# One layer, two mixers: h transposed through DRAM instead of on TensorE, and modulation row 5 at another place

## The chip, the cores and the metric

The kernel runs on one core of a Trainium2 chip. A core has five engines that work side by side: TensorE (PE; its weight loads are listed as PEld), VectorE (DVE), ScalarE (ACT), GpSimd (POOL) and SyncE (SP). SP only issues transfers here, one after the other, and waits wherever a transfer's data or its buffer isn't ready. Each engine works through its own row of instructions in a fixed order; semaphores hold an instruction until what it needs is there. The metric is the device time of one execution in microseconds (us).

## The reference, cut to what matters

One transformer-like layer over 512 tokens of width 1024, in fp32:

```python
mod = silu(c) @ w_ada + b_ada                  # nine modulation rows of 1024
sh1, sc1, g1, sh2, sc2, g2, sh3, sc3, g3 = split(mod, 9)

u = rms_norm(x, ffn1_norm_g) * (1 + sc1) + sh1
x = x + 0.5 * g1 * swiglu(u, ffn1_w_in, ffn1_w_out)

u = rms_norm(x, mix_norm_g) * (1 + sc2) + sh2
z = u @ w_mix + b_mix                          # q,k,v,o,i,f of the mLSTM; q,k,v,f of attention; two gates
h_m = mlstm_chunkwise(silu(causal_conv(q_m, k_m)), v_m, i_m, f_m)      # 4 heads of 256
y_a = sigmoid(o_m) * rms_norm(h_m, mlstm_norm_g)
y_b = forgetting_attention(q_f, k_f, v_f, f_f)                         # 16 heads of 64
merged = sigmoid(g_a) * (y_a @ w_branch_a) + sigmoid(g_b) * (y_b @ w_branch_b)
x = x + g2 * (merged @ w_out)

u = rms_norm(x, ffn2_norm_g) * (1 + sc3) + sh3
x = x + 0.5 * g3 * swiglu(u, ffn2_w_in, ffn2_w_out)
```

Row 5 of the modulation (counted from 0) is `g2`, which is first needed where the product with `w_out` is added to x.

## The kernel before

**Products.** Every fp32 product is made of three: operands are split into a high part (`uh`, `wh`) and a rest (`ul`, `wl`), and `mm3` (lines 140 to 142) adds high by high, rest by high, high by rest. One weight tile of 128 columns goes through these stations: SP loads it (`raw`, line 105, 512 KB, a ring of three buffers that all weights and all `w_ada` loads share), ACT rounds it to `wh` (line 115), DVE subtracts to get `wl` (line 117), and PE uses it in 24 products of 128x512 (`gemm_stat`). The first and second product of each three or the first two of a tile can start once `wh` is there; the third needs `wl`.

**Stages.** Start and first feed-forward part (to about 380 us), the qk products with the convolutions (`qk_conv`, about 400 to 480), the four mLSTM heads (`mlstm_w`, `mlstm_h`, to about 550), sixteen attention heads in steps `fox_s`, `fox_p`, `fox_o` (to about 815), the two branches (`branch`, to about 920), the product with `w_out`, and the second feed-forward part. Between the steps of the heads and of attention other work is laid in by a generator that `advance` moves on: value and key products, fourteen of the gate products (`gate`), and during the last four attention heads the eight `y_a(m)`. What sets the order on each engine is the order in which this is written, and a scheduler that places every instruction by priority when the program is built; the order is fixed before it runs.

**h of the mLSTM.** `mlstm_h` leaves h of a head as 128 tokens by 256 columns (`hn`, two token blocks to a tile), scales it by its norm on DVE (line 1128, sixteen times) and stores it to DRAM (`h_d`, line 1129). `y_a(m)` needs it the other way round, columns on partitions: it loads 128 columns of all tokens (`ht`, line 1342), transposes four blocks on PE (line 1345), scales on ACT (line 1347) and multiplies with the tanh of the output gate `th` (line 1340) on DVE (line 1348).

**Transposes through DRAM.** The attention's q and k already go another way: DVE transposes every 32x32 block in place (line 1169), the tile is stored, and `blocks` (line 1134) loads it in four transfers of 64 KB that put the blocks at their transposed places.

**Modulation rows.** `ada_row(v, ...)` makes one row in eight steps: a step loads 128 rows of `w_ada` (512 KB through the `raw` ring) and multiplies and adds them on DVE (line 315 first, then 317). Six short pieces (`fold`, `high`, `low`, `total`, `bias`, `put`) follow, each due a number of ticks later; `later` keeps them, `tick` counts. Before, the generator `self.ada` makes rows 5, 6 and 7: row 5 in the second half of `y_a`, a tick and a step at each of its two pauses from m = 4 on, rows 6 and 7 in the branches.

**Gates.** `gate` writes the tanh of a gate (`tg`, line 1364) and stores it to `g_d` (line 1366); the branches load it back (line 1374). `post(n, f)` keeps a piece of program back for n steps of `advance`.

**Start.** In the first product's loop the modulation of block n is summed in pieces; `mod_first(n)` is its first multiply, on ACT (line 838), or on DVE if its second argument is true (line 836). `lo()` in `u_part` makes the `ul` of a norm (line 281).

Of the kernel before, what the change touches and what calls it, by code (L numbers as in the profile page):

```python
# [20 lines left out]
P = 128  # L21
# [26 lines left out]
class Layer:  # L48
# [35 lines left out]
    def advance(self, gen, n):  # L84
        for _ in range(n):
            next(gen, None)
            for p in self.posts[:]:
                p[0] -= 1
                if p[0] < 0:
                    self.posts.remove(p)  # L90
                    p[1]()
# [179 lines left out]
    def u_part(self, hf, b, k, pool, G, sh, act, eng):  # L271
# [7 lines left out]
        else:  # L279
            pin(nc.vector.tensor_scalar(uf, ps, G[:, k:k + 1], sh[:, k:k + 1], op0=MUL, op1=ADD))  # L280
        return lambda: pin(eng.tensor_tensor(self.ul[k][:, c], uf, self.uh[k][:, c], op=SUB))  # L281

# [495 lines left out]
    def start(self, st, tp):  # L778
# [131 lines left out]
        for k in range(NK):  # L910
# [13 lines left out]
            if n < NK:  # L924
# [7 lines left out]
                if n + 1 < NK:  # L932
                    mod(n + 1, 6, 8)
                    w_hi(n + 1)
                    if n + 2 < NK:
                        mod_first(n + 2)
                    w_lo(n + 1)
# [165 lines left out]
    def mlstm_h(self, h, ip):  # L1103
        nc, sp = self.nc, self.sp
        (Wh, Wl), (vh, vl) = self.W[h], self.vt[h]
        ss = sp.tile([P, NT], F32, name=self.nm("hs"), tag="hs", bufs=2)
        hs = []
        for tb in range(NT):
            if tb % 2 == 0:
                h2 = ip.tile([P, 2, 256], F32, name=self.nm("hn"), tag="bc", bufs=4)  # L1110
            ps = self.tbank()
            for sb in range(tb + 1):
# [14 lines left out]
        for tb in range(NT):  # L1127
            nc.vector.tensor_scalar(hs[tb], hs[tb], r[:, tb:tb + 1], None, op0=MUL)
            nc.sync.dma_start(self.h_d[tb * P:(tb + 1) * P, h * 256:(h + 1) * 256], hs[tb])

# [194 lines left out]


    def y_a(self, m, ap, ip):
        nc = self.nc
        def step():
            if m >= NK // 2:  # L1330
                self.tick()
                next(self.ada)
        ps = self.gbank()
        w = self.w_stat(self.A["w_mix"][0], OM + m * P)
        self.gemm_stat(ps, w, 0, T, range(0, 4))
        step()
        yield
        self.gemm_stat(ps, w, 0, T, range(4, 8))
        th = self.tmp(ip, "th")
        nc.scalar.activation(th, ps, AF.Tanh, scale=0.5, bias=self.hom[:, m:m + 1])  # L1340
        ht = ip.tile([P, NT, P], F32, name=self.nm("ht"), tag="tok", bufs=4)
        nc.sync.dma_start(ht, self.h_d[:, m * P:(m + 1) * P].rearrange("(b p) n -> p b n", p=P))
        b = self.tbank()
        for tb in range(NT):
            nc.tensor.transpose(b[:, tb * P:(tb + 1) * P], ht[:, tb, :], self.ident)
        ya = ap.tile([P, T], F32, name=self.nm("ya"), tag="qk", bufs=16)
        nc.scalar.activation(ya, b, AF.Copy, scale=self.hmg[:, m:m + 1])
        nc.vector.scalar_tensor_tensor(ya, th, 1.0, ya, op0=ADD, op1=MUL)
        self.ya[m] = ya
        step()  # L1350
        yield


    def gate(self, m, i, ip, th=None):
# [10 lines left out]
        if not keep:  # L1365
            nc.sync.dma_start(self.g_d[8 * i + m], th)
        yield
# [26 lines left out]
    def run(self):  # L1394
# [140 lines left out]
        row = lambda: yp.tile([2, 512], F32, name=self.nm("br"), tag="qk", bufs=16)  # L1535
        self.ada = (s for v in (5, 6, 7) for s in self.ada_row(v, new, row, self.gbank))
        with tc.tile_pool(name="gates", bufs=1) as mp:
# [3 lines left out]
            for m in range(4, 8):  # L1541
                ps = self.gbank()
                self.gemm_stat(ps, self.w_stat(w_mix, m * P), 0, T)
                if m == 7:
# [3 lines left out]
        with tc.tile_pool(name="att", bufs=1) as ip:  # L1548
# [149 lines left out]
```

## Time and profile before

| | |
|---|---|
| median of 3 runs | 1315.86 us (1315.68 to 1318.32) |
| the profiled execution | 1316.01 us |
| its span, first to last instruction | 1314.2 us |
| granted TensorE clock, mean | 0.999 |
| PE busy | 1296.7 us |
| DVE busy | 960.1 us |
| ACT busy | 631.6 us |

How to read the rows shown below. In the page's first part, each engine has its busy time, its share of the span and its number of instructions. A row of the windows has the stretch in us, then for each engine its busy time and how many instructions lie there, then the clock, the share of the DMA engines and GB/s. A row of the chain has the start, the length and what it was: each piece is what released the one after it. A row of the waits reads "who, line <- for whom: us in total, times, longest". A row of the timeline has start, length, engine, line and operation, out<-in, and in brackets how long the engine stood idle before it and for what. A row of one line or tile has the count, then the shortest, median and longest duration in ns, then the first and last start. In a row of the groups the mean of one is given in ns behind the busy time.

### The profile page before, as it was taken

How to read it: one execution, taken by the hardware profiler on the slowest of the kernel's cores; microseconds unless marked ns; L12 is line 12 of the kernel's file. 1: busy time of each engine (PE TensorE's matmuls, PEld its weight loads, DVE VectorE, ACT ScalarE, POOL GpSimd, SP SyncE). 2: the span in 40 equal slices, each digit the busy share in tenths (PEclk: the TensorE clock that was granted, in tenths of full speed). 3: DMA queues.
4: the chain of work that ended last, by engine and by line, in shares of the span. 5: the costliest groups of instructions: out<-in, count | busy, mean ns of one | idle time of the engine just before them, and what ended most of it. 6: DMA issues, size and time to landing. Idle time of an engine off the chain costs nothing.

```text
span 1314.2 us, 17824 instructions
## 1 busy us (share of the span) xinstructions
PE 1296.7 (99%) x6297; PEld 1087.8 (83%) x6297; DVE 960.1 (73%) x1747; ACT 631.6 (48%) x1056; POOL 36.9 (3%) x57
## 2 busy tenths in 40 slices
PE   7999999999999999999999999999999999999998
PEld 6788888887889888888888878878898888888887
DVE  6877777578688687888888679677557556635787
ACT  5633232355476555567575766234372223223642
POOL 1000000000010101000000000003000000000000
PEclk9999999999999999999999999999999999999999
DMA  9999888465845334535545467777639777634574
GB/s 289 277 328 302 298 275 275 152 192 160 299 134 141 110 107 130 165 117 137 141 115 168 109 188 203 216 247 234 189 101 322 265 246 262 215 103 133 171 266 148
DMA packets 231563, 260.49 MB, mean 198 GB/s; under 512 B 40545, under 2 KB 172289, under 8 KB 231473
## 3 DMA queue, kind: packets, MB, share of 16 engines
q1 hardware_dynamic: 231088, 259.27, 63.3%
q8 instruction: 50, 0.82, 0.3%
q14 instruction: 41, 0.33, 0.1%
q0 software_dynamic: 320, 0.06, 0.0%
q10 hardware_dynamic: 64, 0.02, 0.0%
HBM read 220.43 MB, written 38.87 MB: 197 GB/s over the span
## 4 chain that ended last, share of the span: by engine, by line
PE 83%; DVE 6%; DMA 5%; ACT 3%; issue 2%; SPq 1%; DVEq 0%; ACTq 0%
PE g L142 21%; PE g L141 21%; PE g L140 21%; PE t L140 4%; PE t L141 4%; PE t L142 4%; DMA raw<-in_w_branch_a_dram 2%; PE g L922 1%; DMA raw<-in_w_mix_dram 1%; DVE wl L117 1%; ACT wh L115 1%; PE t L1320 1%; DVE acc L317 1%; PE t L1290 1%; PE t L1261 1%
## 5 line engine op out<-in xcount | busy, mean ns | idle before, releaser
L115 ACT ACTIVATE wh<-raw 128x1024 fp32r<-128x1024 f32 (+2 forms) x246 | 249.0, 1016 | 376.1 <-PE g L141 107.2
L117 DVE TENSOR_TENSOR wl<-raw,wh 128x1024 fp32r<-128x1024 f32 (+2 forms) x246 | 288.0, 1173 | 164.2 <-ACT wh L115 142.3
L140 PE MATMUL g<-uh,wh 128*128 128x512 f32 (+1 forms) x880 | 340.7, 387 | 0.0
L141 PE MATMUL g<-ul,wh 128*128 128x512 f32 (+1 forms) x880 | 339.4, 386 | 0.8 <-DVE ul L281 0.8
L142 PE MATMUL g<-uh,wl 128*128 128x512 f32 (+1 forms) x880 | 339.4, 386 | 0.0
L141 PEld LDWEIGHTS g<-ul,wh 128*128 128x128 f32 x880 | 165.4, 188 | 33.7 <-DVE ul L281 1.0
L142 PEld LDWEIGHTS g<-uh,wl 128*128 128x128 f32 x880 | 165.3, 188 | 33.7
L140 PEld LDWEIGHTS g<-uh,wh 128*128 128x128 f32 x880 | 165.3, 188 | 32.6 <-issue 0.6
L140 PE MATMUL g<-wh,uh 128*128 128x512 f32 (+1 forms) x256 | 96.6, 379 | 0.0
L141 PE MATMUL g<-wl,uh 128*128 128x512 f32 (+1 forms) x256 | 96.5, 377 | 0.1
L142 PE MATMUL g<-wh,ul 128*128 128x512 f32 (+1 forms) x256 | 96.5, 377 | 0.0
L317 DVE SCALAR_TENSOR_TENSOR acc<-raw,ccol,acc 128x512 f32<-128x512 f32 (+1 forms) x70 | 66.8, 975 | 38.3 <-DMA raw<-in_w_ada_dram 38.1
L140 PE MATMUL t<-wh,A 128*128 128x512 f32 x176 | 68.6, 390 | 0.0
L141 PE MATMUL t<-wl,A 128*128 128x512 f32 x176 | 68.6, 390 | 0.0
L142 PEld LDWEIGHTS g<-wh,ul 128*128 128x128 f32 x256 | 48.2, 188 | 9.1
L141 PEld LDWEIGHTS g<-wl,uh 128*128 128x128 f32 x256 | 48.2, 188 | 8.9 <-DVE wl L117 0.5
L140 PEld LDWEIGHTS g<-wh,uh 128*128 128x128 f32 x256 | 48.1, 188 | 8.4
L142 PE MATMUL g<-yh,wl 128*128 128x512 f32 x128 | 50.1, 391 | 1.2 <-DVE wl L117 1.2
L141 PE MATMUL g<-yl,wh 128*128 128x512 f32 x128 | 49.9, 390 | 0.0
L140 PE MATMUL g<-yh,wh 128*128 128x512 f32 x128 | 49.8, 389 | 0.0
L1272 ACT ACTIVATE S<-S,mn 128x128 f32<-128x128 f32 (+1 forms) x64 | 35.5, 555 | 22.1 <-DVE mn L1264 11.0
L433 ACT ACTIVATE A<-E 128x768 fp32r<-128x768 f32 x22 | 18.6, 845 | 50.9 <-DVE E L432 50.9
(366 smaller groups left out, 2235.5 us busy)
## 6 DMA issues: line engine op xcount, KB each, us to landing
raw<-in_ffn_w_in_dram SPq DMA_DIRECT2D x82, 512.0 KB
raw<-in_w_ada_dram SPq DMA_DIRECT2D x56, 512.0 KB
raw<-in_w_mix_dram SPq DMA_DIRECT2D x46, 512.0 KB
sa<-in_ffn_w_out_dram SPq DMA_DIRECT2D x22, 512.0 KB
sb<-in_ffn_w_out_dram SPq DMA_DIRECT2D x44, 256.0 KB
ws<-sa SPq DMA_DIRECT2D x22, 512.0 KB
ws<-sb SPq DMA_DIRECT2D x44, 256.0 KB
raw<-ws SPq DMA_DIRECT2D x44, 256.0 KB
```

The source lines that it names most:

```text
L115: nc.scalar.activation(hi, src, AF.Copy)
L117: self.last_lo = nc.vector.tensor_tensor(lo, src, hi, op=SUB)
L140: pin(mm(ps, lh, rh, start=start, stop=False))
L141: pin(mm(ps, lh, rl, start=False, stop=False))
L142: self.last_mm = pin(mm(ps, ll, rh, start=False, stop=stop))
L317: nc.vector.scalar_tensor_tensor(a, r[:, s], c, a, op0=MUL, op1=ADD)
L433: nc.scalar.activation(A1[:, 0:3, :], E[:, 0:3, :], AF.Copy)
L922: pin(nc.tensor.matmul(acc_ps[b], (wl if p == 1 else wh)[:, b % 2, s], self.ul[k] if p == 2 else self.uh[k], start=k == 0 and p == 0, stop ...
L1261: nc.tensor.matmul(ps[:, :w], q[:, s], k[:, :w], start=True, stop=False)
L1272: nc.scalar.activation(S[:, ws], S[:, ws], AF.Exp, scale=-1.0, bias=m, accum_out=sm[:, qb:qb + 1])
L1290: tr = lambda b, c, qb, kb: nc.tensor.transpose(b[:, c:c + P], S[:, P_OFF[qb] + kb * P:P_OFF[qb] + (kb + 1) * P], self.ident)
L1320: nc.tensor.matmul(po[:, q0:], vt[:, kb, i, :], Px[:, o:o + T - q0], start=n == 1, stop=n == 8)
```

## The change

h of the mLSTM is scaled on ACT, transposed on DVE in 32x32 blocks (two token blocks at a time, 128x512), and stored so; `ht_load` brings it with `blocks`, one m ahead of its use, and `y_a` has no PE transposes. Row 5 gets a generator of its own, `early`: four steps beside the qk products m = 4 to 7, four in the mLSTM heads 0 and 1; `advance` now ticks on each step that was really taken. Its sums lie in `yb[5]` to `yb[7]`, which are not yet in use there. A gate's store, h's store and ya's last operation are posted one step later. At the start, for n = 1, `mod_first` goes to DVE and comes after `w_lo`. `lo()` notes `last_ul`, so that the first multiply of row 8 is placed behind the last `ul` of the second feed-forward part's norm.

```diff
@@ advance
-            next(gen, None)
+            if next(gen, self) is not self:
+                self.tick()
@@ u_part
-        return lambda: pin(eng.tensor_tensor(self.ul[k][:, c], uf, self.uh[k][:, c], op=SUB))
+        def lo():
+            self.last_ul = pin(eng.tensor_tensor(self.ul[k][:, c], uf, self.uh[k][:, c], op=SUB))
+        return lo
@@ start
                     w_hi(n + 1)
+                    if n == 1:
+                        w_lo(n + 1)
+                        mod_first(n + 2, True)
+                        continue
                     if n + 2 < NK:
                         mod_first(n + 2)
                     w_lo(n + 1)
@@ mlstm_h
-            nc.vector.tensor_scalar(hs[tb], hs[tb], r[:, tb:tb + 1], None, op0=MUL)
-            nc.sync.dma_start(self.h_d[tb * P:(tb + 1) * P, h * 256:(h + 1) * 256], hs[tb])
+            nc.scalar.activation(hs[tb], hs[tb], AF.Copy, scale=r[:, tb:tb + 1])
+            if tb % 2:
+                t = h2s[tb // 2].rearrange("p b n -> p (b n)")
+                nc.vector.transpose(t, t)
+                self.post(1, lambda t=t, b=tb - 1: nc.sync.dma_start(
+                    self.h_d[b * P:(b + 2) * P, h * 256:(h + 1) * 256].rearrange("(b p) n -> p b n", p=P),
+                    t.rearrange("p (b n) -> p b n", b=2)))
@@ y_a
+    def ht_load(self, m, ip):
+        t = ip.tile([P, T], F32, name=self.nm("ht"), tag="tok", bufs=4)
+        self.blocks(t, self.h_d[:, m * P:(m + 1) * P])
+        self.ht.append(t)
+
     def y_a(self, m, ap, ip):
         nc = self.nc
-        def step():
-            if m >= NK // 2:
-                self.tick()
-                next(self.ada)
+        if m == 0:
+            self.ht = []
+            self.ht_load(0, ip)
         ps = self.gbank()
         w = self.w_stat(self.A["w_mix"][0], OM + m * P)
         self.gemm_stat(ps, w, 0, T, range(0, 4))
-        step()
         yield
+        if m + 1 < NK:
+            self.ht_load(m + 1, ip)
         self.gemm_stat(ps, w, 0, T, range(4, 8))
         th = self.tmp(ip, "th")
         nc.scalar.activation(th, ps, AF.Tanh, scale=0.5, bias=self.hom[:, m:m + 1])
-        ht = ip.tile([P, NT, P], F32, name=self.nm("ht"), tag="tok", bufs=4)
-        nc.sync.dma_start(ht, self.h_d[:, m * P:(m + 1) * P].rearrange("(b p) n -> p b n", p=P))
-        b = self.tbank()
-        for tb in range(NT):
-            nc.tensor.transpose(b[:, tb * P:(tb + 1) * P], ht[:, tb, :], self.ident)
         ya = ap.tile([P, T], F32, name=self.nm("ya"), tag="qk", bufs=16)
-        nc.scalar.activation(ya, b, AF.Copy, scale=self.hmg[:, m:m + 1])
-        nc.vector.scalar_tensor_tensor(ya, th, 1.0, ya, op0=ADD, op1=MUL)
+        nc.scalar.activation(ya, self.ht[m], AF.Copy, scale=self.hmg[:, m:m + 1])
+        self.post(1, lambda: nc.vector.scalar_tensor_tensor(ya, th, 1.0, ya, op0=ADD, op1=MUL))
         self.ya[m] = ya
-        step()
         yield
@@ gate
-            nc.sync.dma_start(self.g_d[8 * i + m], th)
+            self.post(1, lambda: nc.sync.dma_start(self.g_d[8 * i + m], th))
@@ run
-        self.ada = (s for v in (5, 6, 7) for s in self.ada_row(v, new, row, self.gbank))
+        early = self.ada_row(5, lambda: self.yb[6:8], lambda: self.yb[5][0:2, :], self.tbank)
+        self.ada = (s for v in (6, 7) for s in self.ada_row(v, new, row, self.gbank))
...
             for m in range(4, 8):
                 ps = self.gbank()
-                self.gemm_stat(ps, self.w_stat(w_mix, m * P), 0, T)
+                w = self.w_stat(w_mix, m * P)
+                next(early)
+                self.gemm_stat(ps, w, 0, T)
...
-                    advance(fill, n)
+                    for _ in range(n):
+                        advance(fill, 1)
+                        if f == self.mlstm_w and h < 2:
+                            next(early, None)
```

How the rows of the engines move, at the places of which the prediction speaks. First SP where `y_a` begins, at about 740 to 755 us. `ht` of the lowest number is h for `y_a(0)`; the first `raw` holds the weights of `y_a(1)`; `tg` are gates on their way to `g_d`, and `A` is for the attention. Before:

```order
375 L1134 DMA fT_7113<-t_d_87 32x16x32 x4
376 L1366 DMA g_d_100<-tg_7201 128x512
377 L1366 DMA g_d_101<-tg_7265 128x512
378 L1366 DMA g_d_102<-tg_7311 128x512
379 L1342 DMA ht_7479<-h_d 128x4x128
380 L105 DMA raw_7518<-in_w_mix_dram 128x8x128
381 L1366 DMA g_d_103<-tg_7401 128x512
382 L1250 DMA A_1427_7536<-A_d 128x512
383 L1342 DMA ht_7580<-h_d 128x4x128
```

And now:

```order
385 L1378 DMA g_d_100<-tg_7249 128x512
386 L1378 DMA g_d_101<-tg_7313 128x512
387 L1147 DMA ht_7482<-h_d 32x16x32 x2
388 L1378 DMA g_d_102<-tg_7359 128x512
389 L1378 DMA g_d_103<-tg_7449 128x512
390 L1147 DMA ht_7482<-h_d 32x16x32 x2
391 L1147 DMA ht_7518<-h_d 32x16x32 x4
392 L106 DMA raw_7568<-in_w_mix_dram 128x8x128
393 L1263 DMA A_1438_7587<-A_d 128x512
```

The weights of `y_a(1)` stood ahead of the last gate's store and behind one load of h; they stand behind both last gates' stores and eight loads of h.

The row of ACT a little later, around `th` of `y_a(1)` (`Ph`, `Pl`, `S` and `yt` belong to the attention; the `wh` are the weights of later `y_a`). Before:

```order
640 L115 ACTIVATE wh_7605<-raw_7603 128x1024
641 L1285 ACTIVATE Ph_7626<-ident 128x128
642 L1272 ACTIVATE S_7540,sm_7542<-S_7540,mn_7541 128x128
643 L115 ACTIVATE wh_7706<-raw_7704 128x1024
644 L1272 ACTIVATE S_7540,sm_7542<-S_7540,mn_7541 128x256
645 L1272 ACTIVATE S_7540,sm_7542<-S_7540,mn_7541 128x384
646 L1272 ACTIVATE S_7540,sm_7542<-S_7540,mn_7541 128x512
647 L1340 ACTIVATE th_7578<-g_7517,hom 128x512
648 L1347 ACTIVATE ya_7587<-t_7582,hmg 128x512
```

And now:

```order
651 L116 ACTIVATE wh_7570<-raw_7568 128x1024
652 L1298 ACTIVATE Ph_7675<-ident 128x128
653 L1285 ACTIVATE S_7591,sm_7593<-S_7591,mn_7592 128x128
654 L1285 ACTIVATE S_7591,sm_7593<-S_7591,mn_7592 128x256
655 L1285 ACTIVATE S_7591,sm_7593<-S_7591,mn_7592 128x384
656 L1285 ACTIVATE S_7591,sm_7593<-S_7591,mn_7592 128x512
657 L1360 ACTIVATE ya_7717<-ht_7617,hmg 128x512
658 L1358 ACTIVATE th_7634<-g_7567,hom 128x512
659 L116 ACTIVATE wh_7653<-raw_7651 128x1024
```

Before, the weights of two later `y_a` were rounded ahead of this `th`; now those of the next one come right behind it.

DVE at the end of the norm of the second feed-forward part, at about 970 to 980 us; `acc` is row 8's first multiply. Before:

```order
1417 L281 TENSOR_TENSOR ul_9304<-uf_9541,uh_9296 128x256
1418 L281 TENSOR_TENSOR ul_9305<-uf_9545,uh_9297 128x256
1419 L315 TENSOR_SCALAR acc_9790<-raw_9791,ccol 128x1024
1420 L281 TENSOR_TENSOR ul_9306<-uf_9549,uh_9298 128x256
1421 L281 TENSOR_TENSOR ul_9307<-uf_9553,uh_9299 128x256
```

And now:

```order
1426 L283 TENSOR_TENSOR ul_9287<-uf_9530,uh_9279 128x256
1427 L283 TENSOR_TENSOR ul_9288<-uf_9534,uh_9280 128x256
1428 L283 TENSOR_TENSOR ul_9289<-uf_9538,uh_9281 128x256
1429 L283 TENSOR_TENSOR ul_9290<-uf_9542,uh_9282 128x256
1430 L318 TENSOR_SCALAR acc_9771<-raw_9772,ccol 128x1024
```

The multiply went from the middle of the last eight `ul` to behind them.

More of the change, by code (lines that the diff above doesn't have):

```diff
@@ L1106, in mlstm_h @@
         ss = sp.tile([P, NT], F32, name=self.nm("hs"), tag="hs", bufs=2)
-        hs = []
+        hs, h2s = [], []
         for tb in range(NT):
@@ L1110, in mlstm_h @@
                 h2 = ip.tile([P, 2, 256], F32, name=self.nm("hn"), tag="bc", bufs=4)
+                h2s.append(h2)
             ps = self.tbank()
```

## The prediction

> **What bounds the kernel.** I read the page's busy shares first, then TensorE's busy time by windows of 20 us, then, where a window is not full, the chain and the waits there.
>
> ```profile
> PE 1296.7 (99%) x6297; PEld 1087.8 (83%) x6297; DVE 960.1 (73%) x1747; ACT 631.6 (48%) x1056; POOL 36.9 (3%) x57
> core 0: us, PE busy (x) PEld busy (x) DVE busy (x) ACT busy (x) POOL busy (x), PEclk, DMA share, GB/s
> 400.00:420.00 20.00, 20.00 (x140) 18.99 (x139) 18.39 (x35) 13.70 (x19) 0.40 (x4) 1.00 0.63 177
> 420.00:440.00 20.00, 20.00 (x91) 16.26 (x91) 17.45 (x24) 14.04 (x19) 1.02 (x3) 1.00 0.37 107
> 760.00:780.00 20.00, 17.79 (x94) 14.93 (x94) 15.79 (x50) 13.55 (x31) 0.00 (x0) 1.00 0.66 193
> 860.00:880.00 20.00, 18.71 (x82) 14.84 (x81) 13.88 (x22) 7.59 (x11) 1.59 (x1) 1.00 0.79 259
> 960.00:980.00 20.00, 19.16 (x156) 18.72 (x155) 12.91 (x31) 16.91 (x34) 0.00 (x0) 1.00 0.31 99
> ```
>
> TensorE (PE) is the bound: 1296.7 of 1314.2 us, at clock 1.00 in these windows. So only two things move the time: matrix work taken off PE, and holes in PE's row of work, opened or closed. All the holes together are 17.5 us. The three that the change touches are 2.2 us (window 760:780), 1.3 us (860:880) and 0.8 us (960:980). The chain ahead of the first, and those ahead of the other two:
>
> ```profile
> 767.29 3.97 DMA raw<-in_w_mix_dram
> 771.28 1.07 ACT wh L115
> 772.37 1.23 DVE wl L117
> 773.86 0.50 PE t L1261
> ...
> 875.16 1.23 DVE wl L117
> 876.43 0.50 PE g L142
> ...
> 972.09 5.16 DMA raw<-in_w_ada_dram
> 977.34 0.76 DVE acc L315
> 978.10 0.34 DVE ul L281
> 978.49 0.38 PE g L141
> ```
>
> Each is a load that comes late and drags a piece of VectorE (DVE) work behind it: at 773.86 y_a's weights (raw, then wh, then wl); at 876.43 a branch weight's wl; at 978.49 the subtraction ul that stands in DVE's row behind the first multiply of modulation row 8, which waits for its own load.
>
> **The change, part by part.**
>
> *PE transposes gone.* One set in y_a:
>
> ```profile
> 753.59 0.60 PE L1345 MATMUL t<-ident,ht 128*128 128x128 f32 x4
> 754.02 1.26 PE L1290 MATMUL t<-ident,S 128*128 128x128 f32 x10
> 755.03 0.48 PE L140 MATMUL g<-uh,wh 128*128 128x512 f32 x1
> 755.34 0.40 PE L141 MATMUL g<-ul,wh 128*128 128x512 f32 x1
> ```
>
> Starts tell the pace: four take 754.02 - 753.59 = 0.43 us. (Ten from 754.02 to 755.34, less one product's 0.23, are 1.09, so 0.109 each; four of them 0.44.) Eight sets: **-3.5 us**, on the path, since PE is full around them.
>
> [...]
>
> *What replaces them, in mlstm_h.* Rows of the same operations:
>
> ```profile
> L1128 DVE TENSOR_SCALAR hn<-hn,rq 128x256 f32<-128x256 f32 x16 | 5.5, 407 | 0.1
> L1122 ACT ACTIVATE hj<-hn x16: 401/418/420, 480.8 to 544.1; 128x256 f32<-128x256 f32 x16
> L1169 DVE STREAM_TRANSPOSE tk<-tk 128x512 f32<-128x512 f32 x12 | 7.8, 687 | 0.0
> ```
>
> DVE loses 16 multiplies, 5.5 us, and gains 8 transposes at 0.687, also 5.5. ScalarE (ACT), busy for 48% of the span, gains 16 x 0.42 = 6.7 us in the four mlstm_h, whose Squares (L1122) run from 480.8 to 544.1. Nobody reads h before y_a, 200 us later. Cover: that distance. If a transpose waits on ACT it holds the DVE row behind it, at most 16 x 0.42 spread over four heads; the other bound is a little below nothing, as the two engines now share the tail. I take 0, bounds -0.4 to +1.
>
> *Row 5 moved.* Eight w_ada loads and their sums leave y_a's second half for 400 to 490:
>
> ```profile
> L317 DVE SCALAR_TENSOR_TENSOR acc<-raw,ccol,acc x70: 731/750/1780, 68.8 to 1094.4; 128x512 f32<-128x512 f32 x42, 128x1024 f32<-128x1024 f32 x28
> DVE acc L317 <- DMA raw<-in_w_ada_dram: 38.1, 17, 7.0
> raw<-in_w_ada_dram SPq DMA_DIRECT2D x56, 512.0 KB
> 404.33 1.22 DVE L117 TENSOR_TENSOR wl<-raw,wh 128x1024 fp32r<-128x1024 f32 x1
> 414.37 0.48 PE L140 MATMUL g<-uh,wh 128*128 128x512 f32 x1
> ```
>
> A step is two halves of 0.75, so 1.5 us of DVE, plus a wait: 38.1 us over 56 loads is 0.7 us on average, 7.0 at worst. Four steps go beside the qk gemms, where DVE is 18.39 and 17.45 of 20 busy: 4.2 us free in 40, and the four ask 4 x (1.5 + 0.7) = 8.8. The 4.6 us over come out of the lead that wl has on PE: 414.37 - (404.33 + 1.22) = 8.8 us. It holds, so 0; the other four steps stand in the first heads and go by the same lead. Bounds: 0 and, at the longest waits, 4 x 8.5 - 4.2 - 8.8 = +21; I stay at the low end, as the mean wait is the nearer row, and price the middle below as a rival.
>
> *y_a without row 5.* The 3.97 us load at 767.29 waited for a raw buffer (there are three) while w_ada loads used them too. Without these the weights load earlier, and the hole at 773.86 closes: **-2.2 us**.
>
> *Order on SP at y_a's start.* Before, the weights of y_a(1) were issued at 740.63, ahead of the last gate store. Now they stand behind two gate stores, which wait for their tanh, and behind six more block loads of h:
>
> ```profile
> 740.63 0.55 SPq L105 DMA_DIRECT2D raw<-in_w_mix_dram  x1
> 749.92 0.33 SPq L1366 DMA_DIRECT2D g_d<-tg  x1
> ...
> 746.22 0.40 ACT L1272 ACTIVATE S<-S,mn 128x128 f32<-128x128 f32 x1 [2.65 <-DVE mn L1264]
> 747.71 0.72 ACT L1238 ACTIVATE fk<-fT,colA 64x512 fp32r<-64x512 f32 x1
> 749.20 0.69 ACT L1364 ACTIVATE tg<-g,hgg 128x512 f32<-128x512 f32 x1
> 751.41 0.59 ACT L1323 ACTIVATE yt<-t 64x512 f32<-64x512 f32 x1
> ...
> L1134 SPq DMA_DIRECT2D fT<-t_d x48: 318/487/1437, 594.5 to 728.1; - x48
> 812.63 3.77 DMA raw<-in_w_branch_a_dram
> ```
>
> On ACT the new order is: first S (746.22 + 0.40, ends 746.7 with its sum read out), two fk (0.72 each, of which the row shows one), yt 0.59, tanh 0.69, a second S, wider than the first (0.7, an estimate from the first's 0.40 and its read-out), last tanh 0.69. That ends at 750.8. The store is issued by 751.1. Six block loads at 0.49 (the same loads of fT): 754.0. The weights land 3.8 us later, 757.8; wh 1.07 and wl 1.23 make it 760.1. PE asks for y_a(1) on the same clock as follows:
>
> ```profile
> 745.45 0.28 PE L1261 MATMUL t<-fk,fq 128*128 128x256 f32 x1
> ...
> 746.74 0.40 PE L140 MATMUL g<-uh,wh 128*128 128x512 f32 x1
> ```
>
> Before at 755.03; now one set of transposes less (-0.44) and one head's S products more ahead of it (746.74 - 745.45 = 1.29): 755.9; its third product, the first that needs wl, 0.46 later, 756.3. 760.1 - 756.3 = **+3.8 us**, a new hole. Bounds: 0 (if SP gets there early) and 5.5 (a load as slow as the 5.16 above).
>
> *wh behind th.* In the new ACT order the wh of a later m mostly stands behind th(m), which waits for gemm m's end. From there th (0.69, as the tanh above), wh 1.07 and wl 1.23 must pass while PE has S (1.29), an attention product or ten transposes (1.09), and the two products (0.46) that don't need wl: 2.99 against some 2.4 to 2.9, short by about 0.1 to 0.5 each time if nothing else lies between; where wh still comes ahead of th, nothing. Of seven I count one full shortfall, **+0.5 us**; bounds 0 and 7 x 0.47 = 3.3. The last operation of ya goes a step later; nothing reads ya before the branch part.
>
> *Branch part.* It keeps rows 6 and 7, in the same order on SP, so its hole comes from inside it; it is now entered with loads ahead. I take half of 1.3, **-0.7**, bounds -1.3 and +1.
>
> *Row 8's first multiply* now stands behind all eight ul: the 0.8 at 978.49 goes, **-0.8**. It costs nothing later: DVE is 12.91 of 20 busy there.
>
> *Start.* One multiply goes from ACT to DVE:
>
> ```profile
> PE t L856 <- DVE ac L841: 1.0, 2, 0.7
> ```
>
> PE waits there for DVE's own sums, and the moved one stands behind w_lo(2): 0, bounds -0.7 and +0.5. The gate stores themselves keep their places on SP nearly everywhere else: 0.
>
> **Sum.** -3.5 - 2.2 + 3.8 + 0.5 - 0.7 - 0.8 = -2.9 us. The profiled execution took 1316.01, so 1313.1; the median of the runs, 1315.86, lies 0.15 under it, so **1313.0 us**.
>
> **Rivals.**
> - *A, no hole at y_a(1).* If the stores and block loads pass SP quickly, the 3.8 us are not paid: -6.7, **1309.2 us**. For it: the tanh could run earlier on ACT when its fk wait less. Against: SP's order is fixed and the last gate's tanh cannot start before its gemm ends at 745.4.
> - *B, slower: row 5 starves the convolutions.* A multiply that waits for its w_ada load holds DVE, and the wl behind it. Four steps with a wait of w ask 4 x (1.5 + w) and have 4.2 + 8.8 = 13.0, so it decides from w = 1.8 us. The trace has a mean of 0.7 and a longest of 7.0. At 3.25 the hole is 6 us: +3.1, **1319.0 us**. For it: only three raw buffers, shared half and half. Against: in the branch part the same one-to-one mix costs only 1.3 us.
> - *C, nothing gained.* The y_a stage is held by the chain of load, wh and wl, not by PE; what PE saves on transposes is waited for instead. That is 3.3 in place of 0.5 for wh behind th: -0.1, **1315.8 us**. For it: the hole at 773.86 has that form.
>
> **How the numbers follow.** My forecast has 0.44, with its own range 1310.4 to 1315.5 (the bounds of the y_a(1) hole and of the branch part); A 0.22, B 0.18, C 0.16. A change under 0.2% (2.6 us) can't be told from none here. The forecast lies just past it: 0.28 of it is faster, 0.16 same. A is all faster, B all slower, C spreads 0.04, 0.06 and 0.06. So faster 0.54, same 0.22, slower 0.24. The range takes in A and B but for their outer ends: 1307.5 to 1319.0.
>
> **What would show it.** No transposes of ht on PE, and 753 to 815 without the 2.2 us hole. A PE wait of 3 to 5 us for y_a(1)'s wh or wl, with SP's raw issue near 754 behind two gate stores. No PE wait for ul near 977. PE full from 400 to 490; if DVE's acc waits there for w_ada more than 1.8 us a step and PE waits for wl, B is right. Wrong altogether I would be if the new holes lie where no order moved.

## The result, and the profile after

The changed kernel takes 1320.28 us (median; 1318.83 to 1322.75) against 1317.3 for the kernel before on the same chips (1315.14 to 1318.76). The ratio is 1.0023, with an interval of 1.0016 to 1.003: slower by 0.23%, some 3 us. The forecast was 1313.0, faster. It has the wrong sign, and the time lies outside the range.

The profiled execution of after took 1320.28, its span is 1318.5. The one of before (1316.01) lies 1.3 us under its own median, so the two traces differ by 4.3 us where the medians differ by 3.0. The busy row of the page of after:

```profile
PE 1299.0 (99%) x6265; PEld 1087.6 (82%) x6265; DVE 959.6 (73%) x1740; ACT 638.1 (48%) x1071; POOL 38.0 (3%) x57
```

PE has 32 instructions fewer, the transposes, and is busy 2.3 us longer. The windows of after, in the columns that the prediction shows:

```profile
400.00:420.00 20.00, 20.00 (x137) 18.83 (x136) 18.55 (x37) 13.16 (x18) 0.40 (x4) 1.00 0.63 170
420.00:440.00 20.00, 20.00 (x91) 16.31 (x90) 19.18 (x28) 14.41 (x20) 1.24 (x3) 1.00 0.54 156
...
460.00:480.00 20.00, 18.12 (x81) 14.59 (x82) 18.09 (x36) 14.38 (x31) 1.03 (x2) 1.00 0.37 111
...
760.00:780.00 20.00, 16.92 (x68) 13.28 (x69) 10.25 (x28) 8.77 (x19) 0.00 (x0) 0.83 1.07 205
780.00:800.00 20.00, 19.76 (x105) 16.66 (x105) 16.23 (x50) 15.26 (x36) 0.00 (x0) 1.00 0.35 70
800.00:820.00 20.00, 18.94 (x91) 15.28 (x90) 10.34 (x16) 8.88 (x15) 0.00 (x0) 1.00 0.35 86
860.00:880.00 20.00, 20.00 (x90) 16.57 (x89) 14.76 (x23) 8.44 (x13) 0.00 (x0) 1.00 0.66 216
960.00:980.00 20.00, 20.00 (x152) 18.91 (x151) 13.80 (x35) 17.31 (x35) 0.00 (x0) 1.00 0.19 61
```

PE is now full at 860 and at 960, where it had holes. The convolutions, 400 to 440, stay full. New holes stand at 460 and between 780 and 820, and at 760 the hole is deeper than before and the granted clock falls to 0.83.

Laying the same PE instruction of both traces side by side gives the ledger, after less before: -0.9 us until the end of the convolutions (458), +3.1 in the first heads, 0 through attention to 747, **+5.0 in the y_a stage**, -1.8 in the branches, -1.1 at the norm of the second feed-forward part; together +4.3, as the executions. From here on the length of a hole is the distance of two starts on PE less their usual pace. It comes out some 0.17 us longer than the idle time in the brackets of the rows: the hole at 773 in before is 2.4 by this measure and 2.2 in the brackets.

**The first heads.** First the window of before, then the chain of after that leads to the new holes:

```profile
460.00:480.00 20.00, 20.00 (x100) 17.02 (x99) 14.58 (x32) 11.68 (x27) 1.04 (x2) 1.00 0.40 119
```

```profile
449.24 7.14 DMA raw<-in_w_ada_dram
...
456.48 1.21 DVE yb L320 x2
...
458.47 1.79 DVE yb L320
460.25 0.61 DVE vf L1066
...
464.50 0.61 DVE vf L1066
465.11 0.04 issue
465.15 0.50 PE g L141
```

And the waits there, 455 to 482:

```profile
DVE yb L320 <- DMA raw<-in_w_ada_dram: 2.7, 1, 2.7
...
PE g L141 <- DVE vf L1066: 1.8, 2, 1.0
```

Row 5's multiplies (`yb`) wait 2.7 us for a `w_ada` load of 7.14 us and then take 3.78 us in a row, two steps together. Behind them in DVE's row stands `vf`, which empties the bank that the value product was written to. PE's next product into such a bank waits for it: holes of 1.17, 0.29 and 0.92 us between 459.8 and 465.2, 2.4 of the 3.1 us.

**The start of y_a.** SP's row, the row of PE, and ACT's row at the end of the stage:

```profile
751.76 1.40 SPq L1378 DMA_DIRECT2D g_d<-tg  x2
753.21 3.14 SPq L1147 DMA_DIRECT2D ht<-h_d  x6
756.40 0.49 SPq L106 DMA_DIRECT2D raw<-in_w_mix_dram  x1
```

```profile
757.99 0.39 PE L1274 MATMUL t<-fk,fq 128*128 128x256 f32 x1 [0.66 <-DVE Pl L1302]
...
759.27 0.40 PE L1275 MATMUL t<-klz,fq 128*128 128x512 f32 x1
762.12 0.80 PE L141 MATMUL g<-uh,wh 128*128 128x512 f32 x1 [2.46 <-ACT wh L116]
762.71 0.63 PE L142 MATMUL g<-ul,wh 128*128 128x512 f32 x1
764.31 0.79 PE L143 MATMUL g<-uh,wl 128*128 128x512 f32 x1 [0.96 <-DVE wl L118]
764.90 0.63 PE L141 MATMUL g<-uh,wh 128*128 128x512 f32 x1
765.32 0.63 PE L142 MATMUL g<-ul,wh 128*128 128x512 f32 x1
...
769.49 0.39 PE L141 MATMUL g<-uh,wh 128*128 128x512 f32 x1
769.71 0.39 PE L142 MATMUL g<-ul,wh 128*128 128x512 f32 x1
```

```profile
813.04 0.69 ACT L1358 ACTIVATE th<-g,hom 128x512 f32<-128x512 f32 x1 [3.90 <-PE g L143]
813.63 1.05 ACT L116 ACTIVATE wh<-raw 128x1024 fp32r<-128x1024 f32 x1
```

The order on SP is the one forecast: two gate stores, six block loads of `ht`, then the weights of y_a(1), at 756.40. The first product waits for `wh` (762.12), the third for `wl` (764.31). Then something comes that the forecast does not have. Products start 0.43 us apart (764.90 to 765.32) where 0.22 is usual (769.49 to 769.71), until about 768.9. The other rows show the two smaller additions: PE waits for `Pl` at 757.99, a piece of DVE's work on the attention, and late in the stage `wh` comes right behind `th`, which waits 3.90 us for the end of PE's product. Measured as the distance of PE's starts from their usual pace, idle and slow time in the stage are 3.1 us in before and 11.5 in after: +8.4, less the 3.5 us of transposes that are gone, +4.9.

### The profile page after: what moved, and what is told of

Its sections match the earlier page's. It is cut to its first block, busy times and chain, and to the rows that moved or that the text cites. A ratio compares the mean times of both kernels' runs of the same rounds, so it can differ in the third digit from the quotient of the medians.

```text
span 1318.5 us, 17782 instructions
## 1 busy us (share of the span) xinstructions
PE 1299.0 (99%) x6265; PEld 1087.6 (82%) x6265; DVE 959.6 (73%) x1740; ACT 638.1 (48%) x1071; POOL 38.0 (3%) x57
## 4 chain that ended last, share of the span: by engine, by line
PE 79%; DVE 8%; DMA 6%; ACT 3%; issue 2%; SPq 1%; POOL 0%; DVEq 0%; ACTq 0%; POOLq 0%
PE g L143 21%; PE g L142 20%; PE g L141 20%; PE t L141 4%; PE t L143 4%; PE t L142 4%; DMA raw<-in_w_ada_dram 2%; DMA raw<-in_w_branch_a_dram 1%; ACT wh L116 1%; DVE wl L118 1%; PE g L925 1%; PE t L1333 1%; PE t L1303 1%; DMA raw<-in_w_mix_dram 1%; PE t L1274 1%
## 5 line engine op out<-in xcount | busy, mean ns | idle before, releaser
L143 PEld LDWEIGHTS g<-uh,wl 128*128 128x128 f32 x880 | 165.8, 188 | 37.1 <-DVE wl L118 3.4
L320 DVE SCALAR_TENSOR_TENSOR acc<-raw,ccol,acc 128x1024 f32<-128x1024 f32 (+1 forms) x56 | 56.9, 1031 | 38.0 <-DMA raw<-in_w_ada_dram 37.8
```

What stands on the lines that cost most here:

```text
L143: self.last_mm = pin(mm(ps, ll, rh, start=False, stop=stop))
L320: nc.vector.scalar_tensor_tensor(a, r[:, s], c, a, op0=MUL, op1=ADD)
```

## The experiments

"y_a stage" below is the time from the first S product of attention head 12 to the first product of the branches on PE. It is 79.3 us in before and 84.3 in after. The theory on trial: (T) the loss sits on the path load, `wh`, `wl` at y_a's start, made late by SP's row, and in the heads behind row 5. The rivals are named where they are tested.

**One part alone.** Three kernels, each the kernel before with one part of the change.

Row 8 and the start:

```diff
+        def lo():
+            self.last_ul = pin(eng.tensor_tensor(self.ul[k][:, c], uf, self.uh[k][:, c], op=SUB))
+        return lo
...
+                    if n == 1:
+                        w_lo(n + 1)
+                        mod_first(n + 2, True)
+                        continue
```

> The kernel before with two edits alone: the note of the last ul (row 8's first multiply behind it) and the start's mod_first on DVE. My theory: both gain what the changed kernel's trace shows at these places, 1.0 us at 978 and about 0.7 us in the first 60 us: -1.7 us, 0.9987 of before. Rival: the start's gain belongs to run-to-run spread of its first loads, then only -1.0.

Measured: 1316.4 us, ratio 0.9995 (0.9985 to 1.0005). The hole at 978 is gone, 1.0 us; the start's gain can't be told from none. Its trace also shows one thing that can spread the executions of one order, as before's spread over 1314 to 1320 us:

```profile
770.00:775.00 5.00, 2.06 (x14) 1.56 (x12) 2.23 (x4) 2.16 (x3) 0.00 (x0) 1.00 0.49 143
775.00:780.00 5.00, 4.58 (x13) 3.64 (x14) 4.02 (x21) 2.76 (x10) 0.00 (x0) 0.66 0.36 105
```

This edit changes no order near 770, yet the old hole there is 3.5 us long (2.4 in the trace of before) and is followed by 13 products in 5 us at a clock of 0.66. So one and the same order can pay for a hole alone, or for a hole and a slow stretch behind it. The executions agree: of row8_start's ten, the three with a mean granted clock of 1.000 took 1314.75 to 1314.92 us, the seven below it 1316.14 to 1317.89.

Row 5 early, h as before:

```diff
+        early = self.ada_row(5, lambda: self.yb[6:8], lambda: self.yb[5][0:2, :], self.tbank)
...
+                w = self.w_stat(w_mix, m * P)
+                next(early)
...
+                    for _ in range(n):
+                        advance(fill, 1)
+                        if f == self.mlstm_w and h < 2:
+                            next(early, None)
```

> The kernel before with row 5 moved to the convolutions and first heads (and the tick in advance), h still transposed on PE, gates stored at once. My theory: the hole near 461 to 465 comes with it, +3 us there, because vf stands on DVE behind row 5's sums that wait for their loads; y_a's hole of 2.2 us at 773.86 goes, and the branch hole of 1.3 goes too: -0.5 us in all, between -1.5 and +1. Rival: the hole in the heads comes from h's scaling on ACT or from the posted stores; then it is absent here and the sum is -3.5.

Measured: 1315.51, ratio 0.9985 (0.9976 to 0.9995).

```profile
460.00:480.00 20.00, 18.46 (x85) 14.73 (x84) 18.13 (x36) 14.38 (x31) 1.04 (x2) 1.00 0.38 110
...
760.00:780.00 20.00, 19.39 (x103) 16.29 (x102) 16.98 (x50) 14.92 (x33) 0.00 (x0) 1.00 0.98 257
```

The hole in the heads is there without any other part of the change: it belongs to row 5. It is paid back in y_a (a hole of 0.8 in place of 2.4) and in the branches (none in place of 1.4).

h through DRAM as in the change, with h's stores and ya's last operation posted; row 5 stays in y_a, and the gate stores are not posted. The main lines:

```diff
+        if m + 1 < NK:
+            self.ht_load(m + 1, ip)
...
-        for tb in range(NT):
-            nc.tensor.transpose(b[:, tb * P:(tb + 1) * P], ht[:, tb, :], self.ident)
...
+        ya = ap.tile([P, T], F32, name=self.nm("ya"), tag="qk", bufs=16)
+        nc.scalar.activation(ya, self.ht[m], AF.Copy, scale=self.hmg[:, m:m + 1])
```

> The kernel before with h scaled on ACT, transposed on DVE, stored and brought by block loads one m ahead; row 5 stays in y_a, gates are stored at once. My theory: the weights of y_a(1) still stand on SP behind seven block loads and a gate store, so PE has its hole of 3 to 4 us near 760 and runs at about half pace for some 3 us behind it; with the hole at 773 kept in part: +2 to +6 us. Rival: the hole needs the gate stores a step later; then -3.5 for the PE transposes and nothing against it.

Measured: 1331.47, ratio 1.0108 (1.009 to 1.0127), 14 us, far beyond what was expected. The y_a stage is 95.9 us, 16.6 longer than before. One of its windows:

```profile
800.00:820.00 20.00, 15.45 (x66) 11.80 (x64) 10.12 (x15) 5.87 (x10) 0.00 (x0) 0.91 0.63 168
```

So taking the transposes off PE is not only work saved. And the other parts of the change do not add to the loss of this one: with them the stage is 84.3 us, and row 5's move takes most of the loss away again, as a later pair shows.

**Is it the slow clock?** After, with useless transposes laid in ahead of y_a(1)'s first product, to keep PE at work while it would wait:

```diff
+        if m == 1:
+            for _ in range(22):        # 35 in the second kernel
+                nc.tensor.transpose(ps[:, 0:P], self.ident, self.ident)
         self.gemm_stat(ps, w, 0, T, range(0, 4))
```

> The changed kernel with 22 more transposes of the identity on PE (2.4 us of useless work, written to the bank that y_a(1) then overwrites) in the place where PE would stand idle ahead of y_a(1). Clock theory: the first 14 products of y_a(1) ran at 0.43 us instead of 0.23 because PE had been idle; with the idle time filled they run at 0.23, the granted clock stays at 1.00, and the kernel is 2.9 us faster than the changed one although it does more work. Rival: the slow pace has another cause (operands arriving, PSUM); then 0.43 stays and the time is that of the changed kernel or up to 2.4 us more.

> The changed kernel with 35 useless transposes (3.8 us) on PE ahead of head 13's S products, so that of the idle time before y_a(1)'s third product only about 1.5 us is left, in one piece. Clock theory: with 22 of them 2.8 us were left idle within 4 us and 8 products still ran slow; with 35 none does, the granted clock is 1.00 from 760 to 770, and the kernel is 2.5 to 3 us faster than the changed one, about 1317.5. Rival: the pace of 0.43 belongs to the products of y_a(1) or the transfers beside them; then at least 8 of them stay slow and nothing is gained.

Measured: 1319.58 with 22 (1.0018; 1.0009 to 1.0027), 1318.9 with 35 (1.0011; 1.0002 to 1.002). The 22 settle nothing: holes of 1.31 and 1.52 us were left, and the clock still fell behind them, later (to 0.92 in the window from 760 to 765 and 0.74 from 765 to 770). With 35, the windows of after and then of this kernel:

```profile
760.00:765.00 5.00, 1.92 (x4) 1.11 (x5) 2.58 (x9) 1.75 (x4) 0.00 (x0) 0.70 1.10 216
765.00:770.00 5.00, 5.00 (x16) 3.91 (x15) 2.85 (x13) 2.63 (x7) 0.00 (x0) 0.62 1.12 206
```

```profile
760.00:765.00 5.00, 3.76 (x29) 3.23 (x27) 2.35 (x4) 1.55 (x3) 0.00 (x0) 1.00 1.16 245
765.00:770.00 5.00, 4.91 (x22) 4.06 (x23) 3.63 (x20) 3.13 (x9) 0.00 (x0) 1.00 0.70 129
```

One hole of 1.5 us is left, the clock stays at 1.00, and 22 instead of 16 instructions run from 765 to 770. The stage is 82.0 us, 2.4 shorter than in after, though PE does 35 x 0.109 = 3.8 us of useless work more. That the slow products are a second price of the hole is shown by these traces. By the starts in after it is about 2.3 us. By the medians the gain is 1.4 us, and the two intervals of the ratios overlap.

**Who holds SP: the posting, the stores or the block loads?** Three kernels, each after with one edit: gate stores not posted; gate stores issued by ACT; the next y_a's weights issued ahead of its `ht` (y_a(0) issues its own at its start).

```diff
-            self.post(1, lambda: nc.sync.dma_start(self.g_d[8 * i + m], th))
+            nc.sync.dma_start(self.g_d[8 * i + m], th)      # no_post
+            nc.scalar.dma_start(self.g_d[8 * i + m], th)    # act_stores
```

```diff
-        w = self.w_stat(self.A["w_mix"][0], OM + m * P)
+        w = self.yw
...
         if m + 1 < NK:
+            self.yw = self.w_stat(self.A["w_mix"][0], OM + (m + 1) * P)    # weights_first
             self.ht_load(m + 1, ip)
```

> The changed kernel with the gates' stores issued by SP at once, as before, not a step later; all else as changed. My theory: the last two stores wait for their tanh in either place, and y_a(1)'s weights stay behind the last of them and seven block loads: the hole near 760 keeps 3 us or more, time within 1 us of the changed kernel. Rival: the posted stores alone made SP late; then the hole and the slow pace go, and 5 us or more are won.

> The changed kernel with the gates' stores to DRAM issued by ACT behind their tanh instead of by SP one step later, so that SP is not held by them ahead of y_a(1)'s weights. My theory: those weights are issued some 10 us earlier, the hole of 4 us near 762 and the slow pace behind it (2.9 us) go: 1313 or less. Rival: the eight block loads of h and the raw ring hold the weights as well; then the hole shrinks by at most the 1 to 2 us that the stores cost, and the slow pace stays.

> The changed kernel with the weights of each next y_a issued on SP ahead of the block loads of its h. My theory: y_a(1)'s weights are issued 2.1 us earlier (four block loads of 0.53), the hole shrinks from 4.0 to about 1.9 us and is then too short to slow the clock: 5 us less than the changed kernel, about 1315.3. Rival: the clock has nothing to do with the hole's length; then 2 us less and the 0.43 us pace stays.

Measured: no_post 1319.67, ratio 1.0023 (1.0013 to 1.0032); act_stores 1314.01, 0.9978 (0.9969 to 0.9988); weights_first 1317.52, 1.0005 (0.9996 to 1.0014). Posting is not the cause: without it the hole and the slow clock are both there (PE busy 17.66 of 20 us from 760 to 780, clock 0.83). With the stores on ACT, SP's row is:

```profile
737.01 8.03 SPq L1147 DMA_DIRECT2D ht<-h_d  x8
745.08 0.49 SPq L106 DMA_DIRECT2D raw<-in_w_mix_dram  x1
```

The weights of y_a(1) go out at 745.08 instead of 756.40, in spite of the eight block loads ahead of them. PE's wait for their `wh` is gone and the clock stays at 1.00, but 0.70 us for `wl` stays at 759, with 0.94 and 0.25 ahead of it, and 0.62 and 0.70 at 807. Weights first takes away most of the same wait with the stores still on SP (PE busy 18.80 of 20 us from 760 to 780, clock 1.00, against 16.92 and 0.83 in after), but the time is lost again late in the stage:

```profile
800.00:820.00 20.00, 17.75 (x82) 14.16 (x81) 10.79 (x17) 11.54 (x19) 0.00 (x0) 0.95 0.30 78
```

There PE's last product of a y_a ends at 813.96, `th` starts at 813.99, `wh` right behind it at 814.57, then `wl`, and PE's next products wait for these two: holes of 1.88 and 0.70 us, with a slow clock behind them. That is ACT's row and not SP's; it comes back below. The stage takes 78.7 us with the stores on ACT, 81.7 with weights first.

**The same question put to the kernel before.** Only the stores on ACT, nothing else of the change:

```diff
-            nc.sync.dma_start(self.g_d[8 * i + m], th)
+            nc.scalar.dma_start(self.g_d[8 * i + m], th)
```

> The kernel before with nothing changed but the gates' stores, issued by ACT behind their tanh. My theory: it gains the hole of 0.8 us at 684 (SP held by a gate's store), and the hole at 773, which belongs to row 5's loads in the raw ring, stays: -1 us, 0.9993. Rival: SP's waits for the stores matter to y_a's loads here too; then the hole at 773 shrinks as well, -3 us.

Measured: 1312.56, ratio 0.9967 (0.9954 to 0.998): faster than both kernels. SP's waits in before had this row, which is gone, and the window at 760 of the new kernel is full:

```profile
SPq L1366 <- ACT tg L1364: 37.1, 9, 9.1
```

```profile
760.00:780.00 20.00, 20.00 (x112) 17.13 (x111) 13.31 (x39) 12.20 (x28) 0.00 (x0) 1.00 0.37 102
```

SP had stood 37.1 us behind nine gate stores whose tanh wasn't ready. With them on another queue the hole at 773 closes with row 5 still in y_a, and one of 0.75 at 684 closes too. The stage takes 76.9 us. So the old hole was the stores' doing as much as row 5's: taking either away shrinks it to 0.8 us or nothing. It also puts a price on h through DRAM with the stores off SP: 78.7 (act_stores, where row 5 has left the stage) against 76.9 (here, and also with row 5 moved early, as the next kernels show), **1.8 us longer**, in spite of 3.5 us less work on PE. This price rests on one trace of each. By the ratios of the runs, act_stores (0.9978) and before_act_row5 (0.9974) are level, though the first also has row 8's 1.0 us.

**Parts of the change on top of that.** The same kernel with h through DRAM; with row 5 early; with row 8 and the start. The edits are those shown.

> The kernel before with the gates' stores on ACT and h's way through DRAM, row 5 left in y_a. It tells whether h's new way gains its 3.5 us of PE once SP is free. Theory W (wh behind th): ACT's new order and the chain of load, wh and wl leave holes of 4 to 5 us in y_a whatever SP does, so it is slower than before_act_stores by 1 us or more: over 1313.5. Theory Q (the queue alone): with the stores gone y_a has no holes over 0.5 us, and it is 3 us faster than before_act_stores: 1309.5.

> The kernel before with the gates' stores on ACT and row 5 moved to the convolutions and first heads, h on PE. If the stores were what made y_a's weights late, row 5's move has nothing left to gain there and costs its hole in the heads of 3 us, less the branch hole of 1.4: 1.5 us slower than before_act_stores, about 1314. If row 5's loads were a cause of their own, the two gains add: 1311.

> The kernel before with the gates' stores on ACT, row 8's first multiply behind all ul, and the start's multiply on DVE; row 5 stays in y_a and h on PE. My theory: the parts add, -4.4 (stores, as measured) and -0.9 (as measured): 1311.8 or less, the fastest of all. Rival: the 0.9 was noise; then 1312.6, as before_act_stores.

Measured: with h 1324.4, ratio 1.0058 (1.0044 to 1.0072); with row 5 1313.62, 0.9974 (0.9964 to 0.9985); with row 8 and the start 1313.37, 0.9962 (0.9949 to 0.9976). The waits of the first, 745 to 835:

```profile
ACT th L1356 <- PE g L142: 22.4, 8, 6.9
...
PE g L140 <- ACT wh L115: 3.8, 2, 3.1
```

And ACT's row at the longest of them:

```profile
809.39 0.69 ACT L1356 ACTIVATE th<-g,hom 128x512 f32<-128x512 f32 x1 [6.92 <-PE g L142]
...
811.34 1.04 ACT L115 ACTIVATE wh<-raw 128x1024 fp32r<-128x1024 f32 x1
```

The stores are off SP and h through DRAM still costs 12 us. ACT stands 22.4 us in `th`, which waits for PE; `wh` stands behind it; PE waits for `wh`. At 809 the circle is whole: PE's last product starts at 808.96, `th` follows, then `yt`, `ya` and `wh`, and PE's next product starts at 812.43, after the 3.1 us idle of the row above. (In act_stores `th` waits for 18.2 us in sum, but at the same y_a `wh` stands right behind it, at 806.45 and 807.04, and PE has eight attention products meanwhile: its hole is 0.6 us.) So a second mechanism is shown next to SP's queue, the circle of `th` and `wh`, and row 5's move is what softens it: the y_a stage is 88.8 us with row 5 in it and 78.7 without.

With the stores on ACT and the transposes kept on PE, row 5's move has nothing left to gain in y_a (76.9 us both times), keeps its hole in the heads, and comes out level with, or about 1 us above, before_act_stores. Row 8 and the start are level too. Their hole at 978 is gone, 1.0 us, but in the profiled execution others opened at 870, with a slow stretch behind them:

```profile
860.00:880.00 20.00, 17.49 (x68) 13.48 (x67) 15.30 (x23) 7.59 (x11) 1.58 (x1) 0.91 0.77 251
```

Of its five executions two had a mean granted clock of 1.000 and took 1310.3 us; the three with 0.998 took 1313.4 to 1314.2.

**Can row 5 be placed better?** Three kernels: after with the last four steps spread over `mlstm_h` 0, 1 and `mlstm_w` 2, 3; after with the stores on ACT and the last four steps in the first four `fox_s`; and the kernel before with row 5 spread so, row 8 and the start, its transposes kept on PE.

```diff
-                    for _ in range(n):
-                        advance(fill, 1)
-                        if f == self.mlstm_w and h < 2:
-                            next(early, None)
+                    advance(fill, n)
+                    if (f == self.mlstm_h) == (h < 2):     # spread, comb
+                        next(early, None)
...
                     self.fox_s(n, ip)
+                    if n < 4:                              # best
+                        next(early, None)
```

> The changed kernel with the last four steps of row 5 at other places: one behind mlstm_h of heads 0 and 1 and one behind mlstm_w of heads 2 and 3, so that on DVE they come behind the first vf. My theory: the hole of 2.4 us at 461 to 465 goes and y_a stays as it is: 3 us less than the changed kernel, about 1317.3. Rival: DVE is too full from 440 to 540 wherever the steps stand, and the hole appears further on; then no gain.

> The changed kernel with the gates' stores on ACT and the last four steps of row 5 in the first four attention heads (one behind each fox_s) rather than in the mLSTM heads 0 and 1. My theory: it keeps act_stores' gain and loses the hole of 2.2 us at 461 to 465, as DVE has 3 to 5 us of 20 free from 540 to 580: 1311.5 to 1312, 0.996 of before. Rival: as in the spread variants a hole of the same size opens where the steps now stand; then 1314.

> The kernel before with all of the change but h's way through DRAM and the posted stores, and with row 5's last four steps spread as above: row 8's order, the start, row 5 early, h transposed on PE. My theory: -1.8 (row 5 alone, as measured) -3 (no hole in the heads) -0.9 (row 8 and start, as measured): 1311.6, 0.9957 of before. Rival: holes move rather than go; then about 0.998.

Measured: spread 1321.64, ratio 1.0038 (1.0023 to 1.0053); best 1317.52, 1.0005 (0.9996 to 1.0013); comb 1314.1, 0.998 (0.997 to 0.9989). In the first two the holes at 460 are gone (PE busy 20.00 of 20 us from 460 to 480), but others open. A window of spread, and one of best:

```profile
530.00:550.00 20.00, 17.80 (x90) 15.02 (x89) 17.86 (x56) 13.07 (x31) 0.00 (x0) 0.91 0.48 146
```

```profile
680.00:700.00 20.00, 20.00 (x86) 16.09 (x86) 14.04 (x30) 10.48 (x20) 0.00 (x0) 0.85 0.61 160
```

In spread PE waits 2.4 us at 540 for a sum of row 5, which stands on DVE behind a transpose of `hn`, and that behind ACT's three new scalings of `hn`: one part of the change delays the other. In best a hole of 3.2 us ends at 679.6, and the slow clock follows. Two things end together just ahead, at 678.3: a load of weights, and a piece on DVE that had waited 3.6 us for ACT, where a `tg` waited 2.5 us for PE. Which of them PE waited for stays open. Comb has small holes only (0.8 in the 760 window) and, without h through DRAM, is faster than before by 0.2%. No place that was tried is free.

## Why the prediction was wrong, step by step

- **Transposes gone, -3.5.** The work is gone from PE, but it was not 3.5 us of pure load. Next to what replaced it the y_a stage is longer: by 1.8 us with everything else favourable (act_stores against before_act_stores), by 12 and more with row 5 in it. With them gone, and `wh` behind `th` on ACT, PE waits where it had work before. How much of this is the missing transposes and how much ACT's new order stays open: no run changes the order alone. The forecast saw the mechanism (rival C) and counted it too low.
- **What replaces them in mlstm_h, 0.** Right: h_alone, where only h's way has changed, is level with before from 458 to 740.
- **Hole at 773, -2.2.** It went, but row 5 was not the only way to close it: the gate stores on another queue do the same.
- **y_a(1)'s order on SP, +3.8.** The mechanism is as forecast. The weights go out at 756.40, on a row that runs 2.2 us later than before's; less that, 754.2, and 754.0 was forecast. PE's delay there is 2.6 + 0.4 + 1.4 = 4.4 us. Two things behind it had no term: the slow clock, about 2.3, and the wait for `Pl` just ahead, 1.1. The wait for `Pl` belongs to h's way: it is there in h_alone and before_act_h, which change h and leave row 5 in y_a, and not in before and before_act_stores. Why PE meets `Pl` at that place stays open.
- **wh behind th, +0.5.** This term was mis-sized: holes of 0.19, 0.38, 0.24, 0.62 and 0.70 us from 784 to 816 make 2.1, inside its bound of 3.3.
- **Row 5 moved, 0.** *This is the step that failed in kind.* The forecast took wl's lead of 8.8 us as the cover, and the convolutions do stay full. But the "other four steps in the first heads" do not "go by the same lead": there DVE also empties the banks of the value products (`vf`), and that has no such lead: PE's wait for it comes to 1.8 us in after. One wait of 2.7 us was enough, where rival B had asked for 1.8 in each of four steps. B's mechanism is right, 20 us later and with another victim: +3.1.
- **Branch, -0.7, and row 8, -0.8.** Measured -1.8 and -1.1, in the forecast's direction. The branch's part comes with row 5's move: row5_alone has it too. **Start, 0:** -0.9 until 458 in this trace, of which only 0.5 lies before 60 us; the start alone did not show it.

Put together with what was measured, in the order of the ledger: -0.9 + 3.1 + (-3.5 - 2.4 + 4.4 + 2.3 + 1.1 + 2.1, and 1.0 in pieces under 0.15 us or not assigned: +5.0) - 1.8 - 1.1 = +4.3.

The forecast's own range, 1310.4 to 1315.5, does not come out of the bounds that it names, 0 to 5.5 for the hole and -1.3 to +1 for the branch: these give 1308.6 to 1316.4. The measured 1320.28 lies outside both.

Of the rivals, A (no hole at y_a(1)) was wrong as long as the stores stay on SP. C has part of the truth, and B's mechanism has the rest. The forecast's last sentence also fits: part of the loss lies where only row 5's own steps were laid in, next to work whose order was not looked at.

## What to carry to other kernels

Before taking "small" work off a full engine, ask what passes in its shadow: here a product's output, the next weights' rounding and their subtraction, on ACT and DVE, while ACT waits for PE and PE for ACT (22.4 us in `th` and 3.8 for `wh`, before_act_h). A store that waited for its data on the queue that also issues the loads held every load behind it here (SP stood 37.1 us at nine of them in before); putting the fourteen gate stores on another queue, one line, gave more (1312.56 us, ratio 0.9967) than any part of this change alone. When work that waits for a load is put into an engine's row, list all that stands behind it, above all what empties the next engine's output, and not only the neighbour that was in mind (here `vf`, behind a wait of 2.7 us).

## What the runs showed of the hardware

In these traces a hole in PE's row can cost more than its length. Behind some holes PE's products start 0.43 us apart instead of 0.23 (after, from 764.31 on), at a granted clock of 0.50, for 3.41 us (row8_start) or 6.83 (after). The length alone did not decide. It happened after 0.8 and 2.6 us (after), 3.5 in one piece (row8_start), 3.2 (best), 1.3 and 1.5 (22 transposes) and 1.9 and 0.7 (weights_first, at 814). It did not happen after 2.4 in one piece (before), 1.2, 0.3 and 0.9 within 6 us (after, at 460), 1.5 (35 transposes), or 0.9 and 0.7 (act_stores).

What else went with a fall can be read in the traces of before and after: where the hole lay against a fixed grid. The record of the clock begins at 8.81 us in before and at 11.09 in after, at 1.00. In after the fall at 762.02, the rise at 768.85 and the fall at 1318.39 come 220, 222 and 383 times 3.4133 us after that point (750.93 us over 220); in before the one fall, at 1312.70, comes 382 times 3.4133 us after it. Each of the three falls ends a stretch of this grid in which PE was idle for long: 2.35 us ahead of 762.02, and, behind PE's last product, 2.25 ahead of 1312.70 and 3.41 ahead of 1318.39. Below are one stretch of before, then one of after with the two behind it, and the 3.41 us ahead of a fall in row8_start with the 3.41 behind it:

```profile
769.97:773.38 3.41, 1.68 (x12) 1.24 (x10) 1.40 (x3) 2.10 (x3) 0.00 (x0) 1.00 0.43 127
```

```profile
758.61:762.02 3.41, 1.06 (x4) 0.59 (x4) 0.85 (x2) 1.73 (x3) 0.00 (x0) 1.00 1.15 257
762.02:768.85 6.83, 5.77 (x13) 4.08 (x14) 5.42 (x21) 3.37 (x11) 0.00 (x0) 0.50 1.08 200
```

```profile
773.09:776.50 3.41, 1.08 (x5) 0.91 (x6) 2.57 (x9) 2.67 (x7) 0.00 (x0) 1.00 0.26 52
776.50:779.91 3.41, 3.41 (x10) 2.65 (x9) 2.43 (x13) 2.00 (x6) 0.00 (x0) 0.50 0.38 136
```

In before 1.7 us of the hole lie in one stretch and the rest in the next, and the clock stays. In after 2.4 us lie in one stretch, and it falls at that stretch's end, 762.02. In row8_start 2.3 us lie in the 3.41 ahead of the fall at 776.50. No stretch of before or after with less than 2.25 us idle ends in a fall; the most idle of these is the one of before, with 1.73. What happens between 1.73 and 2.25 us these two traces do not show. So a term of the sum that opens holes like these needed a second term for the slow stretch, with a chance of its own, since the grid begins elsewhere in each of the two traces. In after it was about 2.3 us; half a clock for the 3.41 us of row8_start or the 6.83 of after bounds it at 1.7 or 3.4, an estimate from these two.
